# Partial sums of the first projections: added by VectorE, or copied back into PSUM and summed on there by TensorE

## The chip, the cores and the metric

The kernel runs on one core of a Trainium2 chip. The metric is the device time of one launch in microseconds, the median over runs. The engines that matter are TensorE (PE in the rows, with PEld for its weight loads), VectorE (DVE), ScalarE (ACT), and SyncE (SP), which issues the DMA transfers. GpSimd (POOL) has little to do.

## The reference

A trunk of two layers over 512 tokens of width 2048. Each layer modulates a normalised input, makes one wide projection whose columns belong to four token mixers A to D, gates each mixer's output, and projects back:

```
for i in range(DEPTH):                                    # 2 layers
    mod = silu(c) @ w_ada[i] + b_ada[i]                   # 2048 -> 3 * 2048
    shift, scale, gate = split(mod, 3)
    h = rms_norm(x, norm_w[i]) * (1 + scale) + shift      # (512, 2048)
    proj = h @ w_in[i]                                    # 2048 -> 52 column blocks of 128
    q, k, v, z of A, B, C, D = split(proj)
    y_a, y_b, y_c, y_d = window + sink, 2-D neighbourhood, dense + rotary, dilated
    y = concatenate([y_m * silu(z_m) for the four mixers])
    x = x + gate * (y @ w_out[i])                         # 2048 -> 2048
return rms_norm(x, final_norm_w)
```

All arithmetic is float32. A projection is made of float32 products split in a high and a low part (three matmuls for one step).

## The kernel before

Everything is held transposed: features on the partitions, 512 tokens on the free axis. A **step** (`step`, L213) is one 128x128 block of weights against one 128x512 input tile: three matmuls into one PSUM bank (high times high, high times low, low times high). A column block of the input projection (`kA0`, `zC1`, ...; the PSUM tile is `pj0kA0` in layer 0) needs 16 steps, one for each input tile k. There are 8 PSUM banks. Four steps make a **slot** (`slot`, L147). For each slot's weights ACT writes the high part (`wh`) and DVE the low part (`wl`); the weight blocks are laid out in memory in the order of the steps.

In layer 0 the input tiles `hh`/`hl` become ready one after the other: for each k, four tiles of `w_ada` (512 KB each) are fetched and each is reduced by DVE against `cond` (`ada_do`, L251), then `make_h` (L473) runs on DVE and ACT. So the first 16 column blocks of layer 0 are made together (`first_proj`, L495): the k's come in six groups (`GROUPS`, L62: 1, 2, 3, 4, 4 and 2 tiles). The first `KEPT` names hold a PSUM bank through all groups. The others take a bank for one group only and hand their partial sum to SBUF when the group ends (`closed`, L541): in group 0 ACT copies it into the name's half of a `b4` buffer; in groups 2 and 3 (`DEFER`) ACT copies it into a spare tile that DVE adds later (`merge`, L516); in groups 1, 4 and 5 DVE adds the bank to the SBUF tile. After group 5 the name is evacuated from SBUF.

Beside the steps run two kinds of work, placed by generators that are resumed at given positions of later slots. An **evacuation** (`evac`, L717; at most one started per slot, L159) turns a finished column block into what the mixers need: `ev_k` splits a key block for two heads (ACT copies, DVE subtractions), `ev_q`, `ev_v`, `ev_z` likewise. An attention **unit** (`unit`, L955; at most one started per slot, L154) is one head and 128 queries: scores on PE (`s`), minimum on DVE, exponential on ACT, reciprocal on DVE, scaling on ACT (`P`), transposes on PE (`pt`), copy on ACT, subtraction on DVE, and after every second unit the products with the values on PE (`o`). Layer 0 has 128 units.

What a generator may do is decided while the program is built, by counters of free buffers. The ring `b4` has 11 buffers (`BUFS`, L47): `ev_k` goes on only when `2 + RES` = 6 of them are free and takes two (L787), `ev_v` when 4 (mixers A, C) or 5 (B, D) are free and takes one (L794), a pair of units takes two; the partial sums hold one for two names. `open_proj` (L711) starts a new column block only when 3 PSUM banks are free; until then it puts in slots without steps (`idle`, L170), which carry only units and evacuations. `unit_ready` (L944) holds the next unit, and all behind it, until its head's key and value are there.

From group 1 on a scheduler may shift instructions on an engine against one another; each engine then runs its queue in order.

Of the kernel before, what the change touches and what calls it, by code (L numbers as in the profile page):

```python
# [18 lines left out]
F32 = mybir.dt.float32  # L19
F32R = mybir.dt.float32r  # L20
I32 = mybir.dt.int32
AF = mybir.ActivationFunctionType
ALU = mybir.AluOpType
# [22 lines left out]
).split()  # L46
BUFS = {"P": 4, "tmp": 4, "b4": 11, "qs": 6}  # L47
FIRST = (16, 4)
KEPT = 6
RES = 4  # L50
RES_C = 3
ORDERED = 1
# [4 lines left out]
EV = (1, 96, 4, 1, 5)  # L57
K2 = (6, 112)
DEPTH0 = 4
DEFER = (2, 3)  # L60
MERGE = (0, 0, 0, 0, 0, 3)
GROUPS = ((0,), (1, 2), (3, 4, 5), (6, 7, 8, 9), (10, 11, 12, 13), (14, 15))  # L62
NP, TP, LP, VP = (0, 1), (1, 0), (0, 1), (1, 2)
THR = (2000, 1200)
# [47 lines left out]
class Trunk:  # L112
# [98 lines left out]
            self.w_dma(self.wdma)  # L211

    def step(self, key, ps, kt, hh, hl, first, last, post=None, late=None):  # L213
        if callable(ps):
            ps = ps()
        q, i = divmod(len(self.steps), 4)
        h, lo = self.wc[q]
        c = slice(i * 128, (i + 1) * 128)
        mm = self.nc.tensor.matmul
        self.steps.append(key + (kt,))  # L220
        mm(ps, h[:, c], hh, start=first, stop=False)
        if late is None:
            mm(ps, h[:, c], hl, start=False, stop=False)
            mm(ps, lo[:, c], hh, start=False, stop=last)
            if post:
                post()
            return
        mm(ps, lo[:, c], hh, start=False, stop=False)
        late.append(lambda: mm(ps, h[:, c], hl, start=False, stop=last))
        if post:  # L230
            late.append(post)
# [263 lines left out]
    def first_proj(self):  # L495


        nc, p = self.nc, self.p
        names = ORDER[:FIRST[0]]
        part, acc = {}, {}  # L500
        rest = deque(names[KEPT:])
        merges = deque()
        spare = [0]

        def store():

            if len(self.h) > spare[0]:
                spare[0] += 1
                return p.tile([128, 512], F32, name=f"part{self.uid()}", tag="y", bufs=16), None
            if self.r_qs.free:  # L510
                return self.r_qs.get(), self.r_qs.put
            if self.r_P.free > 1:
                return self.r_P.get(), self.r_P.put
            return None

        def merge():  # L516
            _, t, u, rel = merges.popleft()
            nc.vector.tensor_tensor(t, t, u, op=ALU.add)
            if rel:
                rel()  # L520

        while rest:
            b = self.r_b4.get([128, 1024])
            left = [min(2, len(rest))]

            def rel(ring=self.r_b4, left=left):
                left[0] -= 1
                if not left[0]:
                    ring.put()
            for j in range(left[0]):  # L530
                part[rest.popleft()] = (b[:, j * 512:(j + 1) * 512], rel)
        self.w_conv(0)
        self.make_h(0, 0)
        self.rstd = self.rms_keep(self.rstd)

        def opened(n):
            if n not in acc:
                acc[n] = self.new_ps(f"pj0{n}")
            return acc[n]

        def closed(n, gi):  # L541
            end = gi + 1 == len(GROUPS)
            if n not in part:
                if end:
                    self.evq.append(self.evac(0, n, acc.pop(n)))
                return
            t, rel = part[n]
            ps = acc.pop(n)
            while end and any(m[0] == n for m in merges):
                merge()  # L550
            late = store() if gi in DEFER else None
            if gi == 0:
                nc.scalar.activation(t, ps, AF.Copy)
            elif late:
                nc.scalar.activation(late[0], ps, AF.Copy)
                merges.append((n, t, *late))
            else:
                nc.vector.tensor_tensor(t, ps, t, op=ALU.add)
            self.end_ps()
            if end:  # L560
                self.evq.append(self.evac(0, n, t, rel))

        for gi, grp in enumerate(GROUPS):
            if gi == ORDERED:
                self.ordered.close()
            tasks = self.first_tasks(GROUPS[gi + 1]) if gi + 1 < len(GROUPS) else []
            if gi == 1:
                self.start(self.tables())
            run = [(n, k) for n in names for k in grp]
            if MAJOR:  # L570
                run = [(n, k) for k in grp for n in names[:KEPT]] + [(n, k) for n in names[KEPT:] for k in grp]
            nslot = len(run) // 4
            done = 0
            for si in range(nslot):
                steps = []
                for n, k in run[4 * si:4 * si + 4]:
                    first = k == grp[0] and (n in part or gi == 0)
                    last = k == grp[-1] and (n in part or gi + 1 == len(GROUPS))
                    steps.append((("in", 0, n), lambda n=n: opened(n), k, *self.h[k], first, last,
                                  (lambda n=n: closed(n, gi)) if k == grp[-1] else None))  # L580
                self.slot(steps, [] if gi == si == 0 else None)
                upto = len(tasks) * (si + 1) // nslot
                for f in tasks[done:upto]:
                    f()
                done = upto
                for _ in range(MERGE[gi]):
                    if merges:
                        merge()
            while merges and gi + 2 == len(GROUPS) and MERGE[gi + 1] == 0:
                merge()  # L590

    def in_proj(self, l):
        self.h = []
# [613 lines left out]
```

## Time and profile before

| | us |
|---|---|
| median of 3 runs | 1900.63 (1899.38 to 1901.05) |
| the profiled execution | 1899.33 |
| its span | 1897.5 |
| PE busy in the span | 1857.0 (98%) |
| DVE busy | 1358.4 (72%) |
| ACT busy | 1078.4 (57%) |

The profiled execution is 1.3 us under the median and 1.8 us longer than its span. The busy share is an average over the whole program. What a change in one stage is worth is read from that stage: from the waits of the engine that everything else serves, here PE, and from the clock that it was granted there. Matmuls overlap in the rows (a 128x512 one lasts 0.39 us but the next starts 0.23 us later), so that starts, not durations, give the pace.

### The profile page before, as it was taken

Reading aid. Unit: us, or ns where it says so; the run is one execution under the profiler, and the core shown is the slowest. Engines: PE = TensorE matmul, PEld = TensorE weight load, DVE = VectorE, ACT = ScalarE, POOL = GpSimd, SP = SyncE. Lnnn points to the kernel's source line nnn. Section 1 sums busy time; section 2 is a strip of 40 time slices with the busy share of each in tenths; the row PEclk is TensorE's granted clock in tenths of the full one; section 3 lists DMA queues with packets and bytes.
Section 4 is the critical chain, followed back from the end, with each engine's and each line's share of the span. In section 5 each row is a group of like instructions: output and inputs, shape, how many; then the busy total and the mean of one; then the engine's idle time right before and its main releaser. Section 6 shows DMA issues by size and latency. Waiting matters only on the chain.

```text
span 1897.5 us, 26329 instructions
## 1 busy us (share of the span) xinstructions
PE 1857.0 (98%) x9256; PEld 1548.7 (82%) x9256; DVE 1358.4 (72%) x2861; ACT 1078.4 (57%) x2186; POOL 55.5 (3%) x144
## 2 busy tenths in 40 slices
PE   7899999999999999999999999999999999999997
PEld 5588888888888888888778888888888888888887
DVE  7899978788677768977775775577767666655346
ACT  5243457767777776632245773477757666654333
POOL 0110010200000000000000000110000000000000
PEclk8899999999999999999999999999999999999999
DMA  9998454252133335688833334322233342232335
GB/s 341 300 321 287 140 182 146 85 184 82 58 99 103 96 96 192 240 278 312 289 116 137 117 126 138 106 89 89 101 127 125 115 121 95 87 100 89 133 120 181
DMA packets 91459, 291.44 MB, mean 154 GB/s; under 512 B 10208, under 2 KB 17888, under 8 KB 91328
## 3 DMA queue, kind: packets, MB, share of 16 engines
q1 hardware_dynamic: 91328, 289.76, 45.1%
q8 instruction: 73, 1.20, 0.3%
q14 instruction: 58, 0.48, 0.1%
HBM read 278.57 MB, written 11.16 MB: 153 GB/s over the span
## 4 chain that ended last, share of the span: by engine, by line
PE 86%; DVE 5%; DMA 4%; ACT 2%; issue 2%; SPq 0%; DVEq 0%; ACTq 0%
PE pj1o L101 9%; PE o L101 5%; PE s L101 5%; PE pt L101 4%; PE pj0o L101 3%; PE pj0qB L101 2%; PE pj1zA L101 2%; PE pj1zC L101 2%; PE pj0kB L101 2%; PE pj1vB L101 2%; PE pj1kB L101 2%; PE pj1zB L101 2%; PE pj1qB L101 2%; PE pj1vD L101 2%; PE pj0zC L101 2%; PE pj1qC L101 2%
## 5 line engine op out<-in xcount | busy, mean ns | idle before, releaser
L101 DVE TENSOR_TENSOR wl<-wst,wh 128x512 fp32r<-128x512 f32 x556 | 383.9, 692 | 255.6 <-ACT wh L101 222.3
L101 ACT ACTIVATE wh<-wst 128x512 fp32r<-128x512 f32 x556 | 345.5, 626 | 375.0 <-PE pj1o L101 77.5
L101 ACT ACTIVATE P<-P,sm 128x512 f32<-128x512 f32 (+2 forms) x384 | 245.7, 641 | 135.7 <-DVE sm L101 133.8
L101 PE MATMUL s<-b,qs 128*128 128x512 f32 (+2 forms) x512 | 158.2, 390 | 0.2 <-DVE sm L101 0.2
L101 DVE TENSOR_TENSOR b<-pt,b 128x512 fp32r<-128x512 f32 (+2 forms) x256 | 149.4, 584 | 0.8 <-ACT b L101 0.3
L101 DVE CUSTOM_DVE_ANT_0 b<-b,cond,vec 128x1024 f32<-128x1024 f32 x96 | 123.9, 1290 | 26.9 <-DMA b<-wada 26.6
L101 PEld LDWEIGHTS pt<-cst,P 128*128 128x128 f32 x832 | 106.6, 140 | 34.6 <-ACT P L101 1.4
L101 PEld LDWEIGHTS o<-b,b 128*128 128x128 f32 x896 | 124.7, 190 | 12.2 <-DVE b L101 1.7
L101 PE MATMUL pt<-cst,P 128*128 128x128 f32 x832 | 132.4, 272 | 0.9 <-ACT P L101 0.9
L101 ACT ACTIVATE b<-pt 128x512 fp32r<-128x512 f32 (+2 forms) x256 | 129.8, 507 | 2.3
L101 DVE CUSTOM_DVE_ANT_0 b<-b,cond,half 128x1024 f32<-128x1024 f32 x96 | 124.2, 1294 | 6.2 <-DMA b<-wada 5.1
L101 PE MATMUL o<-b,b 128*128 128x256 f32 (+1 forms) x896 | 123.7, 278 | 1.4 <-DVE b L101 1.4
L101 PE MATMUL pj1o<-yh,wh 128*128 128x512 f32 (+1 forms) x304 | 108.6, 357 | 0.0
L101 PE MATMUL pj1o<-yh,wl 128*128 128x512 f32 (+1 forms) x304 | 108.3, 356 | 0.0
L101 PE MATMUL pj1o<-yl,wh 128*128 128x512 f32 (+1 forms) x304 | 108.1, 356 | 0.0
L101 PE MATMUL pj0o<-yh,wl 128*128 128x512 f32 x256 | 100.1, 391 | 0.7 <-DVE wl L101 0.6
L101 PE MATMUL pj0o<-yh,wh 128*128 128x512 f32 x256 | 100.0, 391 | 0.0
L101 PE MATMUL pj0o<-yl,wh 128*128 128x512 f32 x256 | 99.7, 389 | 0.0
L101 DVE TENSOR_TENSOR ot<-o,ot 64x256 f32<-64x256 f32 x109 | 46.0, 422 | 55.9 <-ACT ot L101 54.6
L101 DVE RECIPROCAL sm<-sm 128x1 f32<-128x1 f32 x256 | 41.4, 162 | 61.8 <-ACT P L101 59.1
L101 PEld LDWEIGHTS s<-b,qs 128*128 128x128 f32 x512 | 78.9, 191 | 2.2 <-DVE sm L101 0.4
L101 ACT ACTIVATE P<-s,sm,rq 128x512 f32<-128x512 f32 x64 | 49.8, 778 | 44.2 <-DVE sm L101 43.9
(365 smaller groups left out, 4411.7 us busy)
## 6 DMA issues: line engine op xcount, KB each, us to landing
wst<-w SPq DMA_DIRECT2D x278, 512.0 KB, 3.6
b<-wada SPq DMA_DIRECT2D x192, 512.0 KB, 6.1
T<-btab SPq DMA_DIRECT2D x16, 448.0 KB, 5.3
T<-gtab SPq DMA_DIRECT2D x16, 448.0 KB, 5.1
x<-xT SPq DMA_DIRECT2D x16, 256.0 KB, 5.3
tmp<-xT SPq DMA_DIRECT2D x16, 256.0 KB, 5.4
xs<-xn SPq DMA_DIRECT2D x16, 256.0 KB, 2.5
out<-xn SPq DMA_DIRECT2D x32, 128.0 KB, 1.8
```

Source lines behind the costliest of these rows:

```text
L101: return f(*a, **k)
```

## The change

`KEPT` goes from 6 to 5, so 11 of the first 16 names hand their sums on. These 11 no longer take a bank for each group: two banks (`rot0`, `rot1`) are held through the whole of `first_proj` and serve the 66 (name, group) places in turn. When a place ends, ACT copies its bank into the name's SBUF tile, and then copies the partial sum of the place after next from SBUF into that bank; the matmuls of that place add to what lies there (`first` is None: the first matmul doesn't start a new sum). The additions on DVE, the spare tiles, `DEFER` and `MERGE` are gone. Eleven names hold six `b4` buffers, ten held five.

```
--- before.py
+++ after.py
@@ -46,7 +46,8 @@
 ).split()
 BUFS = {"P": 4, "tmp": 4, "b4": 11, "qs": 6}
 FIRST = (16, 4)
-KEPT = 6
+KEPT = 5
+ROT = 2
 RES = 4
 RES_C = 3
 ORDERED = 1
@@ -57,8 +58,6 @@
 EV = (1, 96, 4, 1, 5)
 K2 = (6, 112)
 DEPTH0 = 4
-DEFER = (2, 3)
-MERGE = (0, 0, 0, 0, 0, 3)
 GROUPS = ((0,), (1, 2), (3, 4, 5), (6, 7, 8, 9), (10, 11, 12, 13), (14, 15))
 NP, TP, LP, VP = (0, 1), (1, 0), (0, 1), (1, 2)
 THR = (2000, 1200)
@@ -218,10 +218,11 @@
         c = slice(i * 128, (i + 1) * 128)
         mm = self.nc.tensor.matmul
         self.steps.append(key + (kt,))
-        mm(ps, h[:, c], hh, start=first, stop=False)
+        resumed = first is None
+        mm(ps, h[:, c], hh, start=bool(first), stop=False, skip_group_check=resumed)
         if late is None:
-            mm(ps, h[:, c], hl, start=False, stop=False)
-            mm(ps, lo[:, c], hh, start=False, stop=last)
+            mm(ps, h[:, c], hl, start=False, stop=False, skip_group_check=resumed)
+            mm(ps, lo[:, c], hh, start=False, stop=last, skip_group_check=resumed)
             if post:
                 post()
             return
@@ -495,29 +496,13 @@
     def first_proj(self):
 
 
-        nc, p = self.nc, self.p
+        nc = self.nc
         names = ORDER[:FIRST[0]]
         part, acc = {}, {}
         rest = deque(names[KEPT:])
-        merges = deque()
-        spare = [0]
-
-        def store():
-
-            if len(self.h) > spare[0]:
-                spare[0] += 1
-                return p.tile([128, 512], F32, name=f"part{self.uid()}", tag="y", bufs=16), None
-            if self.r_qs.free:
-                return self.r_qs.get(), self.r_qs.put
-            if self.r_P.free > 1:
-                return self.r_P.get(), self.r_P.put
-            return None
-
-        def merge():
-            _, t, u, rel = merges.popleft()
-            nc.vector.tensor_tensor(t, t, u, op=ALU.add)
-            if rel:
-                rel()
+        banks = [self.new_ps(f"rot{i}") for i in range(ROT)]
+        order = [(gi, n) for gi in range(len(GROUPS)) for n in names[KEPT:]]
+        place = {e: i for i, e in enumerate(order)}
 
...
-        def opened(n):
+        def opened(n, gi):
+            if n in part:
+                return banks[place[gi, n] % ROT]
             if n not in acc:
                 acc[n] = self.new_ps(f"pj0{n}")
             return acc[n]
 
         def closed(n, gi):
+
             end = gi + 1 == len(GROUPS)
             if n not in part:
                 if end:
                     self.evq.append(self.evac(0, n, acc.pop(n)))
                 return
+            i = place[gi, n]
+            ps = banks[i % ROT]
             t, rel = part[n]
-            ps = acc.pop(n)
-            while end and any(m[0] == n for m in merges):
-                merge()
-            late = store() if gi in DEFER else None
-            if gi == 0:
-                nc.scalar.activation(t, ps, AF.Copy)
-            elif late:
-                nc.scalar.activation(late[0], ps, AF.Copy)
-                merges.append((n, t, *late))
-            else:
-                nc.vector.tensor_tensor(t, ps, t, op=ALU.add)
-            self.end_ps()
+            nc.scalar.activation(t, ps, AF.Copy)
+            if i + ROT >= len(order):
+                self.end_ps()
+            elif order[i + ROT][0]:
+                nc.scalar.activation(ps, part[order[i + ROT][1]][0], AF.Copy)
             if end:
                 self.evq.append(self.evac(0, n, t, rel))
 
@@ -574,20 +557,15 @@
             for si in range(nslot):
                 steps = []
                 for n, k in run[4 * si:4 * si + 4]:
-                    first = k == grp[0] and (n in part or gi == 0)
+                    first = None if n in part and gi else k == 0
                     last = k == grp[-1] and (n in part or gi + 1 == len(GROUPS))
-                    steps.append((("in", 0, n), lambda n=n: opened(n), k, *self.h[k], first, last,
+                    steps.append((("in", 0, n), lambda n=n: opened(n, gi), k, *self.h[k], first, last,
                                   (lambda n=n: closed(n, gi)) if k == grp[-1] else None))
...
-                for _ in range(MERGE[gi]):
-                    if merges:
-                        merge()
-            while merges and gi + 2 == len(GROUPS) and MERGE[gi + 1] == 0:
-                merge()
```

The order of instructions moves with it. On PE, at the end of group 1 (k = 1, 2), before:

```order
L101 MATMUL pj0zA3_536<-hh0_1_333,wl8_439 128x512
L101 MATMUL pj0zA3_536<-hh0_2_402,wh8_438 128x512
L101 MATMUL pj0zA3_536<-hl0_2_403,wh8_438 128x512
L101 MATMUL pj0zA3_536<-hh0_2_402,wl8_439 128x512
L101 MATMUL pj0kA0_280<-hh0_3_492,wh12_553 128x512
L101 MATMUL g1_544<-tmp21_482,t5_411 16x512
L101 MATMUL pj0zC0_557<-hh0_1_333,wh9_463 128x512
L101 MATMUL pj0zC0_557<-hl0_1_334,wh9_463 128x512
L101 MATMUL pj0zC0_557<-hh0_1_333,wl9_464 128x512
L101 MATMUL pj0zC0_557<-hh0_2_402,wh9_463 128x512
```

Now (`rot1` holds the sum of the last name, `kC0`):

```order
L100 MATMUL rot1_246<-hh0_1_334,wh11_519 128x512
L100 MATMUL rot1_246<-hl0_1_335,wh11_519 128x512
L100 MATMUL rot1_246<-hh0_1_334,wl11_520 128x512
L100 MATMUL rot1_246<-hh0_2_397,wh11_519 128x512
L100 MATMUL rot1_246<-hl0_2_398,wh11_519 128x512
L100 MATMUL rot1_246<-hh0_2_397,wl11_520 128x512
L100 MATMUL pj0kA0_283<-hh0_3_489,wh12_550 128x512
L100 MATMUL g1_541<-tmp21_479,t5_406 16x512
L100 MATMUL pj0kA0_283<-hl0_3_490,wh12_550 128x512
L100 MATMUL pj0kA0_283<-hh0_3_489,wl12_551 128x512
```

The first matmul that reads input tile 3 (`hh0_3`) stood ahead of the group-1 steps of `zC0` to `kC0`; it now stands behind all steps of group 1.

On ACT, in group 5 (`wh` is a weight tile, `tmp<-b4` the tanh of a gate's evacuation, `qs` a query tile), before:

```order
L101 ACTIVATE wh62_1749<-wst32_1644 128x512
L101 ACTIVATE qs11_1847<-pj0qA2_306 64x512
L101 ACTIVATE qs12_1848<-pj0qA2_306 64x512
L101 ACTIVATE wh63_1775<-wst32_1644 128x512
L101 ACTIVATE tmp40_1896<-b410_245 128x512
L101 ACTIVATE tmp41_1916<-b410_245 128x512
L101 ACTIVATE tmp42_1939<-pj0vA0_283 128x512
L101 ACTIVATE wh64_1805<-wst33_1692 128x512
L101 ACTIVATE tmp43_1942<-b411_246 128x512
L101 ACTIVATE wh65_1833<-wst33_1692 128x512
L101 ACTIVATE wh66_1865<-wst34_1732 128x512
L101 ACTIVATE tmp44_1968<-b411_246 128x512
```

Now:

```order
L100 ACTIVATE b410_247<-rot0_245 128x512
L100 ACTIVATE rot0_245<-b411_248 128x512
L100 ACTIVATE tmp40_1859<-b410_247 128x512
L100 ACTIVATE b411_248<-rot1_246 128x512
L100 ACTIVATE wh63_1745<-wst32_1627 128x512
L100 ACTIVATE rot1_246<-b412_249 128x512
L100 ACTIVATE b411_248<-rot0_245 128x512
L100 ACTIVATE tmp41_1880<-b411_248 128x512
L100 ACTIVATE rot0_245<-b412_249 128x512
L100 ACTIVATE wh64_1772<-wst33_1675 128x512
L100 ACTIVATE b412_249<-rot1_246 128x512
L100 ACTIVATE tmp42_1903<-b411_248 128x512
```

Between the weight tiles and the evacuations stand a copy out of a bank (`b4..<-rot`) and a copy into it (`rot<-b4..`) for every place.

On PE, late in the input projection of layer 0, where the units of head 0 of mixer D stand (`s`, `pt`, `o` belong to units, `pj0kD2` to a projection), before:

```order
L101 MATMUL pj0kD2_6527<-hh0_3_492,wh172_6399 128x512
L101 MATMUL pj0kD2_6527<-hl0_3_493,wh172_6399 128x512
L101 MATMUL pj0kD2_6527<-hh0_3_492,wl172_6400 128x512
L101 MATMUL pt447_6569<-cst_68,P98_6491 128x128 x4
L101 MATMUL s448_6579<-b4212_6292,qs31_6038 128x512 x2
L101 MATMUL pj0kD2_6527<-hh0_4_579,wh173_6443 128x512
L101 MATMUL pj0kD2_6527<-hl0_4_580,wh173_6443 128x512
L101 MATMUL pj0kD2_6527<-hh0_4_579,wl173_6444 128x512
L101 MATMUL pj0kD2_6527<-hh0_5_644,wh173_6443 128x512
L101 MATMUL pj0kD2_6527<-hl0_5_645,wh173_6443 128x512
L101 MATMUL pj0kD2_6527<-hh0_5_644,wl173_6444 128x512
L101 MATMUL o450_6594<-b4219_6476,b4196_5779 128x256
```

Now, behind the last step of `qD3`:

```order
L100 MATMUL s435_6891<-b4226_6872,qs25_5993 128x512
L100 MATMUL s433_6883<-b4226_6872,qs25_5993 128x512
L100 MATMUL s435_6891<-b4226_6872,qs25_5993 128x512
L100 MATMUL pt437_6902<-cst_68,P97_6885 128x128 x4
L100 MATMUL s438_6908<-b4226_6872,qs25_5993 128x512 x2
L100 MATMUL pt440_6918<-cst_68,P98_6893 128x128 x4
L100 MATMUL s441_6924<-b4226_6872,qs25_5993 128x512 x2
L100 MATMUL pt443_6936<-cst_68,P99_6910 128x128 x4
L100 MATMUL s444_6944<-b4227_6873,qs26_5994 128x512 x2
L100 MATMUL o446_6953<-b4228_6900,b4193_5702 128x256
L100 MATMUL o446_6953<-b4229_6901,b4193_5702 128x256
L100 MATMUL o446_6953<-b4228_6900,b4193_5702 128x256
```

Before, twelve projection matmuls stand between the scores of one unit and those of the next; now the units of the head follow one another with none between them.

## Rows read from the trace of the kernel before

**Rows 1.** The page, part 1 and the clock line of part 2.

```profile
PE 1857.0 (98%) x9256; PEld 1548.7 (82%) x9256; DVE 1358.4 (72%) x2861; ACT 1078.4 (57%) x2186; POOL 55.5 (3%) x144
...
PEclk8899999999999999999999999999999999999999
```

**Rows 2.** Waits of PE, 0 to 400 us: total, times, longest.

```profile
PE pj0kA L101 <- ACT hh L101: 13.1, 6, 5.5
```

**Rows 3.** Waits of PE, 400 to 1898 us, the longest.

```profile
PE pj1kA L101 <- ACT hh L101: 1.6, 1, 1.6
```

**Rows 4.** Windows: PE, PEld, DVE, ACT, POOL busy, PEclk, DMA share, GB/s.

```profile
core 0: us, PE busy (x) PEld busy (x) DVE busy (x) ACT busy (x) POOL busy (x), PEclk, DMA share, GB/s
36.00:39.00 3.00, 1.59 (x7) 0.90 (x7) 2.18 (x5) 1.30 (x3) 0.00 (x0) 1.00 0.97 325
...
60.00:63.00 3.00, 0.00 (x0) 0.00 (x0) 3.00 (x7) 0.00 (x0) 0.00 (x0) 1.00 0.89 209
...
66.00:69.00 3.00, 3.00 (x6) 1.32 (x5) 1.51 (x2) 0.00 (x0) 0.00 (x0) 0.50 1.02 419
...
84.00:87.00 3.00, 2.72 (x7) 2.12 (x7) 2.22 (x4) 0.65 (x2) 0.00 (x0) 0.56 0.94 319
...
680.00:720.00 40.00, 40.00 (x212) 33.70 (x211) 26.56 (x60) 31.24 (x63) 0.00 (x0) 1.00 0.29 90
```

**Rows 5.** Timeline of PE: start, us, operation [idle before].

```profile
64.85 0.80 PE L101 MATMUL pj0kA<-hh,wh 128*128 128x512 f32 x1 [5.48 <-ACT hh L101]
...
67.98 0.63 PE L101 MATMUL pj0zC<-hl,wh 128*128 128x512 f32 x1
68.41 0.63 PE L101 MATMUL pj0zC<-hh,wl 128*128 128x512 f32 x1
```

**Rows 6.** Chain that ended last, in order of time: start, us, what.

```profile
131.63 10.88 PE pj0zA L101 x48
```

**Rows 7.** Groups of instructions, 0 to 360 us: busy, mean ns.

```profile
L101 DVE CUSTOM_DVE_ANT_0 b<-b,cond,half 128x1024 f32<-128x1024 f32 x42 | 55.2, 1313 | 0.5
...
L101 DVE TENSOR_TENSOR b<-pj0zC,b 128x512 f32<-128x512 f32 x12 | 8.2, 686 | 1.1 <-PE pj0zC L101 1.0
```

**Rows 8.** Groups of ACT, 0 to 230 us.

```profile
L101 ACT ACTIVATE wh<-wst 128x512 fp32r<-128x512 f32 x70 | 42.8, 627 | 73.5 <-PE pj0zC L101 19.3 <-PE pj0zA L101 12.1 <-PE pj0qA L101 11.8
L101 ACT ACTIVATE tmp<-b 128x512 f32<-128x512 f32 x7 | 4.4, 631 | 3.7 <-DVE y L101 2.8 <-DVE b L101 0.8
L101 ACT ACTIVATE part<-pj0zA 128x512 f32<-128x512 f32 x7 | 4.2, 597 | 11.7 <-PE pj0zA L101 9.4 <-DVE tmp L101 2.3
```

**Rows 9.** Timeline, 696 to 705 us: attention units between projection steps.

```profile
696.94 0.69 DVE L101 CUSTOM_DVE_ANT_0 P<-s,T 128x512 f32<-128x512 f32 x1
...
697.67 0.72 ACT L101 ACTIVATE P<-P,sm 128x512 f32<-128x512 f32 x1 [0.83 <-DVE sm L101]
...
698.72 0.72 ACT L101 ACTIVATE P<-P,sm 128x512 f32<-128x512 f32 x1 [0.23 <-DVE sm L101]
...
701.31 0.60 PE L101 MATMUL pt<-cst,P 128*128 128x128 f32 x4
...
701.66 0.72 PE L101 MATMUL s<-b,qs 128*128 128x512 f32 x2
...
702.22 0.39 PE L101 MATMUL pj0kD<-hh,wh 128*128 128x512 f32 x1
...
703.59 1.11 PE L101 MATMUL o<-b,b 128*128 128x256 f32 x8
...
704.54 0.39 PE L101 MATMUL pj0kD<-hh,wh 128*128 128x512 f32 x1
```

**Rows 10.** Groups of ACT by form, 600 to 720 us.

```profile
L101 ACT ACTIVATE P<-P,sm 128x512 f32<-128x512 f32 x40 | 28.9, 723 | 19.2 <-DVE sm L101 19.1
...
L101 ACT ACTIVATE b<-pt 128x512 fp32r<-128x512 f32 x18 | 10.5, 586 | 0.1
L101 ACT ACTIVATE b<-pj0kD 64x512 fp32r<-64x512 f32 x14 | 8.2, 589 | 0.2
```

## The prediction

> **What bounds the kernel now.** I read the page first: PE is busy for 1857.0 of the span's 1897.5 us, and its granted clock is below full only in the first three of 40 slices [rows 1]. Next the waits of PE. In the first 400 us it waited 13.1 us in six pieces for an input tile `hh`, the longest 5.5 us [rows 2]; from 400 us to the end no cause costs more than 1.6 us in all [rows 3], and a late window such as 680 to 720 us shows PE without a gap while DVE and ACT have 9 to 13 us of slack [rows 4]. So the kernel runs at PE's pace. DVE time that is taken away is worth something only in the first stage, until about 130 us, where PE waits for DVE's input tiles. Anything that leaves PE without ready work later is paid in full.
>
> The windows show what a wait costs beyond itself. From 60 to 63 us PE does nothing; its next matmul starts at 64.85 after 5.48 us idle, for the first reader of input tile 3 [rows 4, 5]. From 66 to 69 us the granted clock is 0.50, that is 1.2 GHz, and 128x512 matmuls start 0.43 us apart [rows 4, 5] instead of 10.88/48 = 0.227 us at 2.4 GHz [rows 6]. A shorter gap between 36 and 39 us left the clock at 1.00 [rows 4].
>
> **The change, stage one (until about 225 us).** Removed: 30 direct additions and 20 merges, 0.686 us each [rows 7], 34 us of DVE. Added on ACT: 66 copies out and 55 copies in where there were 30 copies out, so 91 more. A copy from a bank takes 0.597 us [rows 8]; into a bank there is no such row, and I take the same: 54 us, on an engine half idle here. A step is 3 x 0.227 = 0.68 us.
>
> (a) The stall at input tile 3. Before, its first reader stood in front of half of group 1; now it stands behind all of it. The 5.48 us go, and with them the slow matmuls: some eight at 0.43 instead of 0.227 and two table matmuls, about 2.6 us. Together 8. Next late is input tile 4, whose wait lies just ahead of the slow window at 84 to 87 us. Ten additions less (6.9 us) bring it earlier if DVE set its pace; the reductions that make it waited 0.5 us for DMA in 42 instructions [rows 7], but the DMA share there is 0.89 to 1.02 [rows 4]. If DVE sets it, 8 us are won; if DMA, about 4. I take -6.
>
> (b) Groups 0 and 1. A bank must be copied out and refilled while the other bank's place runs: 0.60 + 0.60 us and two hand-offs. Two hand-offs and a reciprocal lie between the exponential's end (698.39) and the scaling's start (698.72) [rows 9], so I put 0.33 us for the two as an upper estimate: 1.53 us, and some 1.65 with a weight tile (0.63 [rows 8]) now and then in front. A place of group 1 gives 2 steps, 1.36 us of cover: 11 x 0.3 = 3.3 us, and once the order on ACT puts a refill behind the next place's copy out, 1.3 us. +4.6. Group 0 has copies out alone, as before: 0.
>
> (c) Groups 2 to 4 give 2.04 and 2.72 us of cover against 1.65, or 2.3 with a weight tile in front: +1.
>
> (d) Group 5. Now the gates' evacuations come between. For each place ACT has 0.60 + 0.60, a tanh of 0.63 and half a weight tile of 0.63 [rows 8]: 2.15 us against 1.36 us of PE. 11 x 0.8 = 8.8, less the four steps of `zB1` that the order has moved in between (2.7): +6. At the low end the tanh's wait and cost nothing, 0; at the high end the six query copies ahead of the first place (6 x 0.6) add up, 12.
>
> Stage one: -6 + 4.6 + 1 + 6, about +6, between -8 and +20.
>
> **The change, stage two: what the sixth buffer moves.** Eleven names hold six `b4` buffers instead of five. The key of mixer A (needs 6 free, takes 2) therefore gets its buffers three slots later in the plan, and all units start three slots later. That alone would cost nothing. But keys wait for 6 free buffers and values only for 5, and following the counters through the code the values of the second, third and fourth pair of B's heads now take their buffers before B's first key. That key is split 24 slots later (slot 147 instead of 123), the first unit of B starts 12 slots later, six query tiles stay occupied, finished blocks hold their banks, and `open_proj` finds fewer than three free. It answers with slots without steps: 47 in layer 0 instead of 4. In the order on PE, 21 units then stand with no projection between them: 3 behind `vD0`, 3 behind `vD1`, 4 behind `vD2`, 10 behind `qD3` (head 0 and 1 of D among them, the piece shown with the change), 1 behind `zD2`. Before, nearly every unit had 12 projection matmuls, 2.7 us, beside it, and PE had no gaps [rows 4].
>
> The price of a unit without cover. PE's own part is 0.56 us for scores (701.66 to 702.22), 0.35 for transposes (701.31 to 701.66) and half of 0.95 for values (703.59 to 704.54): 1.4 us [rows 9]. ACT needs 1.77 us from the exponential's start (697.67) to the scaling's end (699.44) [rows 9] and 0.586 for the transposed copy [rows 10], 2.36 us, and a share of the output's copy; so units follow at about 2.6 us when several are open at once. PE idles 1.2 us in each: 21 x 1.2 = 25. From both sides: were the chain hidden down to ACT's bare 2 x 0.723 + 0.586 = 2.03 us, 0.6 each, 13; were units wholly serial (0.56, then 2.5 from minimum to scaling, 0.35, 0.59, 0.69, hand-offs: 5.5), 4.1 each, 86. I take the value nearest to the ACT row, since the rows of the order show the next scores ahead of the last transposes.
>
> To this come the ends. At four stretches PE waits for the last unit's chain (3.4 us from scores to transposes, less one period): 4 x 0.8 = 3. Behind `qD3` the scores of head 0 wait until a key tile of `kD0` is split (two copies of 0.589 [rows 10] and their subtractions, about 2.6 us) and the stretch ends in one more full chain: 4. Units: 25 + 3 + 4 = 32, between 15 and 95.
>
> The clock. Behind `qD3` PE works about 17 of 35 us, in pieces under 1 us. Whether 1.2 GHz is granted there no row shows; at 84 to 87 us, behind the waits for input tile 4, it was 0.56 though PE was busy 2.72 of 3 us [rows 4]. If it falls, a unit's 1.4 us of PE get longer but partly in time that PE waits anyway: 8 x 0.5 = 4, and 2 for the first projections after it. I take +6, between 0 and 25.
>
> Layer 1's plan is the old one, and the work of each instruction elsewhere is the same: 0.
>
> **Sum.** 6 + 32 + 6 = 44, on the profiled execution's 1899.3: 1943. The runs' median lies 1.3 above that execution, well inside the uncertainty of the terms; forecast 1943, for this case alone 1925 to 1962.
>
> **Rivals.**
> - The chain hides better and stage one gains: units at 13 + 3, no clock, stage one -6: 1899 + 10 = 1909 to 1925. For it: DVE and ACT have slack everywhere after 225 us [rows 4].
> - Faster: input tiles 3 and 4 both come early, so that stage one gives back its waits for `hh` after the first (9.6 of 13.1 us [rows 2]) and the slow clock behind them (4), while the 21 units cost under 10, PE finding its transposes ready each time. From a period of 1.8 us on this wins: 1890 to 1896. Against it stands ACT's 2.03 us.
> - No change: neither copies nor lost cover reach PE, 1899 to 1903. The order speaks against it.
> - The two banks make PE stop for a moment at each of 66 places and the clock falls over the first stage: groups 0, 1 and 5 have 80 steps of 0.68 us, which at 1.2 GHz last 1.28: +32 on top of the rest less what hides in waits, 1962 to 1990. Short gaps so far did not do it: at 36 to 39 us PE was busy 1.59 of 3 us and kept 1.00 [rows 4].
> - Units nearly serial: 21 x 4.1 in place of 25: 1999 and more, from 1990.
>
> The Trainium skill, TensorE: Matmul & The Clock Gate, "A second HAM failure mode: psum-queue depth-cycling", tells of a kernel that cycled through PSUM banks and whose brief idles between groups made the clock swing between its levels; this is the fourth rival's mechanism. The trace of before agrees only in that gaps cost clock (0.50 at 66 us), not that brief ones do (1.00 at 36 us); by the rule the time would be the fourth rival's.
>
> **How the numbers follow.** Forecast 0.57, hiding better 0.13, faster 0.07, no change 0.05, clock swinging 0.11, serial 0.07. A range from 1908 to 1977 holds the forecast, nearly all of the first rival and half of the fourth: about 0.8. Within 0.2% (3.8 us, about what a measurement of this kernel can tell from none) is the third rival: 0.05; faster 0.07; slower the rest, 0.88.
>
> **What would show it.** In the profile after: no wait of PE near 60 us; PE waits of some 0.3 us for ACT at places of group 1 and more in group 5; then PE full until layer 0's D blocks, four idle stretches there, the longest about 35 us with PE near half busy, its waits on ACT `P` and DVE; a lower granted clock in it; layer 1 as before. It is wrong if those stretches are absent or PE is near full in them, or if PE's waits in the first 225 us grow past 30 us.

## The result, and the profile after

The changed kernel took 1965.41 us (median of 4 runs, 1961.32 to 1968.07), the kernel before 1900.01 us beside it: ratio 1.034, 95% interval 1.0325 to 1.0356. The forecast was 1943, with a range of 1908 to 1977: slower as forecast, inside the range, and by half as much again as forecast (+65 instead of +43).

The page of the changed kernel, engine totals and clock (answers to [rows 1]):

```profile
PE 1882.8 (96%) x9256; PEld 1560.4 (80%) x9256; DVE 1334.8 (68%) x2811; ACT 1132.0 (58%) x2277; POOL 62.6 (3%) x144
...
PEclk9999999999999888999999999999999999999999
```

The span has grown by 63.5 us (1897.5 to 1961.0), PE's busy time by 25.8. So not quite half of the loss is slower or stretched PE work, the rest waits. Where it lies is read from the start of the first matmul of each stage, before and after:

```
first matmul of                     before    after   later by
value tile of C (slot 69)            235.3    241.9      6.6
first key tile of B                  338.7    341.5      2.8
output projection, layer 0           773.4    832.0     58.6
first tile, layer 1                  968.4   1031.5     63.1
end of the span                     1897.5   1961.0     63.5
```

The value 2.8 flatters: up to there 38 score matmuls had run instead of 44, since the first scores start at 276.7 us and not at 256.2; their work comes later. The first projections lost about 7 us, layer 0's attention about 52 and the turn between the layers 4 to 5; layer 1 lost nothing.

Layer 0's attention first. Waits of PE in the changed kernel from 341 to 832 us (total, times, longest):

```profile
PE pt L100 <- ACT P L100: 14.7, 8, 3.9
PE o L100 <- DVE sm L100: 4.0, 5, 1.2
PE s L100 <- DVE ot L100: 3.7, 4, 1.1
PE pt L100 <- DVE sm L100: 2.9, 3, 1.1
```

All causes sum to 29.3 us; before, the same stretch (338 to 773 us) had 0.4. 17.7 of them lie behind `qD3` (718 to 762 us). They are the waits of a unit's own chain: transposes for the scaled exponential, scores for a released bank. The windows show two pieces around the first read of input tile 3 (68 to 76 us, for further below), the end of the first projections with the banks in use, the whole attention stretch, and the ten units of head 0 and 1 of D (columns as in [rows 4]):

```profile
core 0: us, PE busy (x) PEld busy (x) DVE busy (x) ACT busy (x) POOL busy (x), PEclk, DMA share, GB/s
68.00:72.00 4.00, 2.26 (x9) 1.22 (x7) 1.43 (x3) 3.54 (x7) 0.00 (x0) 1.00 0.09 36
72.00:76.00 4.00, 2.88 (x9) 1.51 (x10) 2.44 (x4) 0.76 (x2) 0.00 (x0) 0.94 0.01 4
200.00:250.00 50.00, 48.21 (x213) 38.87 (x212) 25.89 (x39) 34.20 (x63) 0.00 (x0) 1.00 0.40 133
341.00:832.00 491.00, 461.52 (x2322) 382.36 (x2320) 328.50 (x768) 327.73 (x689) 13.78 (x39) 0.95 0.29 94
718.00:762.00 44.00, 26.30 (x112) 19.48 (x111) 28.63 (x68) 31.62 (x66) 0.00 (x0) 0.69 0.20 56
```

From 718 to 762 us PE is busy for 26.3 of 44 us at a mean clock of 0.69; before, such a window was full at 1.00 (680 to 720 us, [rows 4]). What the low clock does to a unit stands in PE's timeline, at 1.2 GHz and then, ten us later, at 2.4:

```profile
736.21 1.11 PE L100 MATMUL pt<-cst,P 128*128 128x128 f32 x4 [3.95 <-ACT P L100]
736.98 1.20 PE L100 MATMUL s<-b,qs 128*128 128x512 f32 x2
...
748.33 0.66 PE L100 MATMUL pt<-cst,P 128*128 128x128 f32 x4 [0.44 <-ACT P L100]
748.74 0.71 PE L100 MATMUL s<-b,qs 128*128 128x512 f32 x2
```

Scores of 1.20 instead of 0.71 us, transposes of 1.11 instead of 0.66: the same instructions at half the clock. Counted along PE's trace, 20 units of layer 0 stand in four stretches (3, 3, 4 and 10 units) with no projection matmul between the scores of one unit and those of the next; before, no two units stood so.

From the value tile of C to the output projection PE does the same work in both kernels. Its windows there, before and then after (columns as above):

```profile
235.30:773.40 538.10, 536.83 (x2824) 451.65 (x2822) 415.90 (x972) 381.26 (x828) 19.34 (x64) 1.00 0.37 124
```

```profile
241.90:832.00 590.10, 558.95 (x2820) 463.55 (x2819) 408.35 (x957) 387.15 (x828) 25.33 (x64) 0.96 0.33 108
```

So of the 52 us that are lost here, 30 are idle time of PE and 22 are longer busy time.

Now the first projections. Waits of PE from 20 to 262 us, then the longest wait of SyncE's DMA queue from 40 to 100 us, in the changed kernel:

```profile
PE pj0kA L100 <- ACT hh L100: 10.9, 5, 3.5
PE rot L100 <- ACT rot L100: 4.4, 8, 1.4
PE rot L100 <- DVE wl L100: 1.7, 2, 1.1
PE pj0kA L100 <- DVE hl L100: 1.4, 1, 1.4
```

```profile
SPq L449 <- DVE tmp L100: 13.5, 2, 13.3
```

The same wait in the kernel before, which the prediction had not looked at:

```profile
SPq L448 <- DVE tmp L101: 5.0, 1, 5.0
```

The banks' own waits (`rot` for ACT) are only 4.4 us. The input tiles still cost 10.9, and behind them stands SyncE: line 449 writes the table `gtab`, whose data come from a small PE matmul `g`. That matmul now stands behind all of group 1, so SyncE stood 13.3 us at the write (62.0 to 75.3 us), with the loads for the next input tiles and the weights behind it in its queue. In the windows above the DMA share falls to 0.09 and 0.01 there, and PE is busy 2.26 and 2.88 of 4 us.

### The profile page after: what moved, and what is told of

It reads as the page before. It is cut to its first block, busy times and chain, and to the rows that moved or that the text cites. A ratio compares the mean times of both kernels' runs of the same rounds, so it can differ in the third digit from the quotient of the medians.

```text
span 1961.0 us, 26341 instructions
## 1 busy us (share of the span) xinstructions
PE 1882.8 (96%) x9256; PEld 1560.4 (80%) x9256; DVE 1334.8 (68%) x2811; ACT 1132.0 (58%) x2277; POOL 62.6 (3%) x144
## 4 chain that ended last, share of the span: by engine, by line
PE 84%; DVE 6%; ACT 4%; DMA 3%; issue 2%; POOL 0%; SPq 0%; DVEq 0%; ACTq 0%
PE pj1o L100 9%; PE o L100 5%; PE s L100 5%; PE pt L100 5%; PE rot L100 4%; PE pj0o L100 4%; PE pj1zA L100 2%; PE pj1zC L100 2%; PE pj0qD L100 2%; PE pj0kB L100 2%; PE pj0vB L100 2%; PE pj0qB L100 2%; PE pj1zB L100 2%; PE pj1qD L100 2%; PE pj1qB L100 2%; PE pj0vD L100 2%
## 5 line engine op out<-in xcount | busy, mean ns | idle before, releaser
L100 PE MATMUL pt<-cst,P 128*128 128x128 f32 x832 | 137.7, 280 | 17.8 <-ACT P L100 14.7
L100 PE MATMUL o<-b,b 128*128 128x256 f32 (+1 forms) x896 | 130.2, 285 | 8.5 <-DVE sm L100 4.0
```

The source lines that it names most:

```text
L100: return f(*a, **k)
```

## The experiments

**A sixth buffer alone (e1).** The kernel before, additions and all, plus one buffer that is taken, written in one column and never read:

```diff
+        extra = self.r_b4.get([128, 1024])
+        self.nc.gpsimd.memset(extra[:, 0:1], 0.0)
+        t, rl = part["kC0"]
+        part["kC0"] = (t, lambda: (rl(), self.r_b4.put()))
```

> The kernel before with all its VectorE additions and no rotating banks; only a sixth b4 buffer is taken with the part buffers and given back with the last of them. If the plan's shift is the whole loss, the order on PE gets the same stretches without projections and the time is 1952 to 1966, with PE's first 340 us as before (within 2 us). If the copies between ScalarE and the banks cost the time, this stays at 1899 to 1905.

Measured: 1960.26 us, ratio 1.0303 (1.0286 to 1.0321). Its windows of the attention stretch and of its worst part:

```profile
core 0: us, PE busy (x) PEld busy (x) DVE busy (x) ACT busy (x) POOL busy (x), PEclk, DMA share, GB/s
341.00:827.00 486.00, 457.34 (x2298) 379.40 (x2297) 331.91 (x767) 324.00 (x681) 4.00 (x13) 0.95 0.30 104
720.00:740.00 20.00, 11.82 (x39) 8.73 (x40) 11.63 (x28) 12.56 (x27) 0.00 (x0) 0.50 0.16 46
```

PE idles 28.7 us in that stretch, and in the worst 20 us it is granted 0.50 of its clock. Not one bank copy was needed for that: the plan alone carries almost the whole loss.

**The banks with five buffers (e2).** The changed kernel, the eleventh partial sum in a `P` buffer:

```diff
         while rest:
+            if len(rest) == 1:
+                part[rest.popleft()] = (self.r_P.get(), self.r_P.put)
+                break
             b = self.r_b4.get([128, 1024])
```

> The changed kernel, with the eleventh partial sum in a P buffer, so that five b4 buffers are held as before. If the sixth buffer is the only thing that moves the plan, as the prediction has it, the old order comes back and the time is 1900 to 1908. If the build-time counters are right, which put only the first unit of head 0 two slots later here and yet leave 41 more slots without steps, there is a second way into the same plan and the time is 1950 to 1965.

Measured: 1964.36 us, ratio 1.0325 (1.0304 to 1.0346), with 19 units in stretches without projections, ten in a row. The prediction's "what the sixth buffer moves" is therefore enough for the loss and not needed for it. The first unit starts in slot 78 here (76 before, 79 in the changed kernel). I read the second way from the counters: the meter of VectorE's lag, which now misses the additions, lets the reductions start a slot earlier, and these take buffers as well. That reading was not tested by itself.

**The banks with the old plan (e4).** As e2, and mixer A's key may take its buffers at 5 free:

```diff
-        while self.r_b4.free < 2 + RES:
+        while self.r_b4.free < 2 + (3 if m == "A" else RES):
```

> The changed kernel with five b4 buffers held and mixer A's key let in at 5 free buffers instead of 6, so that the first unit starts one slot earlier than before and layer 0 has the old slots without steps. This is the banks alone. If the plan is the whole loss: no stretch without projections, layer 0's attention at full clock, 1897 to 1906. If the copies into the banks cost: 1930 or more.

Measured: 1908.09 us, ratio 1.0034 (1.0021 to 1.0048), 2 us above what was expected. No two units of layer 0 stand without projections between them. From e2 to e4 the time falls by 56 us, by an edit that lets the first unit start in slot 75 instead of 78 and brings back the old slots without steps: that is the price of the plan. The banks themselves cost 7 (1908.1 against 1900.7 beside it).

**RES = 3, with the sixth buffer, and its control (e5, e6).** `RES = 4` becomes `RES = 3` in the changed kernel and in the kernel before.

> The changed kernel, sixth buffer and all, with RES = 3 instead of 4: in both layers a key waits for 5 free buffers and a value for 4. By the counters layer 0 keeps the old slots without steps, though the first unit still starts late. If the overtaken keys are the cause, 1895 to 1906. If the sixth buffer or the late first unit costs by itself, 1930 or more.

> The kernel before with RES = 3, the control of the run above: no stretch without projections in either, so the difference of the two is the price of the banks with the rest alike. By the first 340 us of the changed kernel, 2.8 us later than before, this one is 2 to 4 us faster than the changed one with RES = 3; if the banks pay for themselves it is slower.

Measured: 1917.48 us (ratio 1.0078, 1.0064 to 1.0092) and 1902.23 us (1.0002, 0.999 to 1.0015). The time of e5 lies between its two expectations. The plan is mended with six buffers too and a first unit as late as slot 78, so neither costs tens of us. But the pair differs by 15 us, where 2 to 4 were expected; e11 takes that up.

**Values wait as long as keys (e10).** In the changed kernel, an edit meant to take away the cause that the prediction named:

```diff
-        while self.r_tmp.free < 2 or self.r_b4.free < 1 + (RES_C if m in "AC" else RES):
+        while self.r_tmp.free < 2 or self.r_b4.free < (1 + RES_C if m in "AC" else 2 + RES):
```

> The changed kernel, with values of mixers B and D waiting for 6 free buffers as the keys do, so that they no longer overtake them. By the counters 29 slots without steps in place of 55 (the kernel before has 12). If the overtaking is the whole cause, as the prediction put it, the time is 1902 to 1912. If the plan is only partly mended and each extra slot without steps costs what it did in the changed kernel, 58 us for 43, the 17 extra cost 23: 1925 to 1937.

Measured: 1944.17 us, ratio 1.0221 (1.0205 to 1.0236): above both expectations. Waits and window of its attention stretch:

```profile
PE pt L100 <- ACT P L100: 14.4, 9, 2.4
```

```profile
core 0: us, PE busy (x) PEld busy (x) DVE busy (x) ACT busy (x) POOL busy (x), PEclk, DMA share, GB/s
347.00:814.00 467.00, 448.86 (x2321) 374.68 (x2320) 328.87 (x767) 326.26 (x688) 13.48 (x39) 0.98 0.30 101
```

18 us of waits are left, and the 17 slots too many cost 2.1 us each (1944.2 against 1908.1 of e4) instead of 1.35: a price per empty slot can't be carried from one plan to another. Nor does the run isolate the overtaking. By the counters of its plan, B's first key is back in slot 120 (123 before, 147 in the changed kernel). But the value of B's first pair, which now waits for 6 free buffers too, gets its buffer in slot 144 (107 before), and B's first unit starts in slot 147 (140 before, 152 in the changed kernel). One lateness was put in place of another, and what the overtaking costs by itself is not shown.

**Fillers in the empty slots (e3, e7).** In layer 0's slots without steps, each bank that a unit takes is first written by matmuls that the real ones overwrite:

```diff
+FILL = (4, 3, 3)          # e7: (2, 1, 1)
+    def fill(self, ps, n):     # self.bare: the slot has no steps
+        if self.bare and len(getattr(self, "h", ())) == KT and self.h[-1]:
+            w = self.wc[max(self.wc)][0][:, :128]
+            for _ in range(n):
+                self.nc.tensor.eng.matmul(ps, w, self.h[-1][0], start=True, stop=True)
...
+        self.fill(sp, FILL[0])
         nc.tensor.matmul(sv, q[:, qc], keys(kk[:, 0]), start=True, stop=False)
```

> The changed kernel, and in layer 0's slots without steps each unit's banks are first written by extra matmuls that the real ones overwrite: 4 of 0.227 us ahead of the scores, 3 each ahead of the transposes and the values. They add some 50 us of PE work at most, most of it meant to lie in PE's waits. If the slow clock is what the prediction undersized, the granted clock stays nearer 1.00 from 620 to 765 us and the time falls by 5 to 20 us, to 1945 to 1960. If the clock follows from something else than PE's gaps, or waits alone set the time, the time is 1965 to 1990 and the clock as low as before.

> As the run with fillers, with 2, 1 and 1 extra matmuls in place of 4, 3 and 3: half the added PE work, some 20 us. In the first such run the clock stayed at 1.00 and PE was full, yet the time did not fall, so the fillers took what the waits and the slow clock had cost. If the slow clock cost about 25 us of its own, half the fillers leave the clock near 1.00 and the time falls to 1943 to 1955. If ScalarE's and VectorE's chains set the pace whatever PE's clock, the time stays at 1960 to 1968.

Measured: 1967.61 us (ratio 1.0351, 1.0332 to 1.037) with 182 fillers, 1957.31 us (1.0295, 1.0277 to 1.0314) with 74. Windows of the attention stretch, e3 and then e7 with the ten units:

```profile
core 0: us, PE busy (x) PEld busy (x) DVE busy (x) ACT busy (x) POOL busy (x), PEclk, DMA share, GB/s
343.00:833.00 490.00, 484.46 (x2499) 403.23 (x2497) 329.57 (x767) 326.19 (x688) 13.77 (x39) 1.00 0.28 94
```

```profile
core 0: us, PE busy (x) PEld busy (x) DVE busy (x) ACT busy (x) POOL busy (x), PEclk, DMA share, GB/s
343.00:821.00 478.00, 463.91 (x2389) 382.46 (x2389) 328.49 (x764) 326.07 (x689) 13.77 (x39) 1.00 0.29 97
718.00:762.00 44.00, 38.91 (x195) 27.96 (x194) 33.77 (x76) 34.09 (x71) 0.00 (x0) 1.00 0.19 56
```

With either, the clock is 1.00 throughout, so the low clock came from PE's gaps. The first number of fillers was too many: 182 x 0.227 = 41 us of added work used up what it saved, and its expected gain did not come. The time with 74 lies between its two expectations. The lighter run gives the price: PE is busy 463.9 us, 74 x 0.227 = 16.8 of them fillers, so 447.1 for the kernel's own work, against 461.5 in the changed kernel. By this estimate the slow clock cost 14.4 us; the same subtraction for e3 (484.5 - 41.3 = 443.2) gives 18. The stretch itself is 12.3 us shorter than without fillers (490.5 to 478.2), while PE did 16.8 us more; 8 us of it reach the end (1965.4 to 1957.3).

**The table's write on another queue (e8, e9).** The two writes of `gtab` are issued by GpSimd, in e4's kernel and in the kernel before:

```diff
-            nc.sync.dma_start(self.gtab[:, :, cs], ...
+            nc.gpsimd.dma_start(self.gtab[:, :, cs], ...
```

> The kernel with the banks and the old plan (five b4 buffers, mixer A's key let in at 5 free), with the two large writes of the table gtab issued by GpSimd instead of SyncE. In the changed kernel SyncE stood 13.3 us at such a write, whose data waits for a PE matmul that stands behind all of group 1, with the reductions' and weights' loads queued behind it, and the DMA share fell to 0.09 and 0.01 at 68 to 76 us. If that is where the first projections lost their time, the waits for input tiles 4 and 5 fall from 6.8 us to under 2 and the time is 1900 to 1905, 4 to 7 below the same kernel with SyncE. If the copies' hand-offs cost the time, it stays at 1906 to 1909.

> The kernel before with the two writes of gtab issued by GpSimd. Here SyncE stood 5.0 us at one of them, before the 5.5 us stall of PE for input tile 3 and the slow clock behind it. If that wait makes the stall, the time is 1891 to 1896, faster than the kernel before. If the loads themselves are the limit there (DMA share 0.89 to 1.02), 1898 to 1902.

Measured: e8 1896.71 us (ratio 0.997, 0.9956 to 0.9983), 11.4 below the same kernel with SyncE (e4, 1908.09) and faster than expected; e9 1895.58 us (0.9962, 0.995 to 0.9974). Windows and PE's waits of e8 in the places shown above:

```profile
core 0: us, PE busy (x) PEld busy (x) DVE busy (x) ACT busy (x) POOL busy (x), PEclk, DMA share, GB/s
68.00:72.00 4.00, 4.00 (x19) 3.17 (x18) 3.84 (x6) 3.58 (x7) 1.57 (x2) 1.00 1.03 314
72.00:76.00 4.00, 4.00 (x19) 3.29 (x19) 4.00 (x6) 2.48 (x5) 2.57 (x2) 1.00 1.02 412
```

```profile
PE pj0kA L100 <- ACT hh L100: 5.7, 3, 3.5
PE rot L100 <- ACT rot L100: 5.3, 6, 1.4
```

The DMA share is 1.03 and 1.02 instead of 0.09 and 0.01, PE is full there, and the waits for input tiles are 5.7 instead of 10.9 us (e4 has the same 10.9), while the banks' waits are no smaller (5.3). So what the first projections lost there was SyncE's stop, not the copies. In e9 the 5.48 us stall for input tile 3 is gone; in its place PE waits 2.3 us at `g`:

```profile
PE pj0kA L101 <- ACT hh L101: 8.9, 5, 3.5
PE g L101 <- DVE b L101: 2.3, 1, 2.3
```

Both runs beat both kernels, the kernel before by 0.3 and 0.4%.

**The sixth buffer again, with the queue free (e11, e12).** e5 and e6 with the same edit:

> The changed kernel with its sixth buffer, RES = 3, and the two writes of gtab issued by GpSimd. With RES = 3 alone it took 1917.5, 15 us more than the kernel before with RES = 3, where 2 to 4 were expected. If SyncE's stop at the write is most of that, as it was with five buffers (1908.1 to 1896.7), the time is 1901 to 1908. If the sixth buffer and the late first unit cost the 15 us, it stays at 1912 to 1918.

> The control: the kernel before with RES = 3 and the two writes issued by GpSimd. RES = 3 changed nothing in the kernel before and the write 5 us, so 1894 to 1898; the run above is then slower by what the banks and the sixth buffer cost when SyncE is out of the way, 4 to 10 us if the late first unit costs, 0 to 3 if it does not.

Measured: 1901.17 us (ratio 0.9996, 0.9987 to 1.0005) and 1895.43 us (0.9958, 0.9944 to 0.9971). Of e5's 15 us too many, the queue's write was most: 5.7 are left, and 1.1 with five buffers (e8 against e9). The trace of e11 has a wait of PE, at 259 us, that e8 and e12 don't have (e5 has it with 3.4 us). It is a likely part of the 5.7, which was not tested:

```profile
PE kb L100 <- POOL rq L295: 3.8, 1, 3.8
```

## Why the prediction was right, and where it was off

The 63.5 us by which the span grew are 6.6 in the first projections, 30 of idle PE and 22 of longer busy PE in layer 0's attention, and 4.5 at the turn between the layers. Forecast were 6 in the first projections, 32 of idle PE, 6 for the clock and nothing at the turn.

**Units without cover: right in the idle time, short in the busy time.** 25 + 3 + 4 = 32 us of idle PE were worked out from the order; 29.3 were measured, 17.7 of them behind `qD3` (18 is what "17 of 35 us" leaves), and half for ACT `P`. 21 units were read from the order, 20 found in the trace. e1, e2 and e4 show that this is the plan's and nearly independent of the banks. What the sum left out is that PE's own work takes longer without cover, whatever the clock: in e7, at full clock, the window from the value tile of C to the output projection has 563.5 us of busy PE, less 16.8 of fillers 546.7, against 536.8 before.

```profile
241.60:821.20 579.60, 563.51 (x2893) 465.47 (x2892) 408.83 (x956) 386.00 (x828) 25.25 (x64) 1.00 0.32 110
```

These 10 us have a likely source in [rows 9]: scores and transposes last 0.72 and 0.60 us, of which the prediction counted 0.56 and 0.35, up to the start of the next matmul. With nothing behind them the whole counts: 20 x 0.41 = 8, an estimate.

**The clock: the term that was mis-sized.** "I take +6, between 0 and 25." The mechanism stood there, and the stretch of ten units, "17 of 35 us", came out as 26.3 of 44 with the clock at 0.69. e7 prices the low clock at 14 us. The step that failed was "partly in time that PE waits anyway". Had the stretched time lain in waits, the waits would have grown by as much when e7 took it away. But e7's idle time and its fillers make 14.1 + 16.8 = 30.9 us, against 29.5 us of idle time in the changed kernel: hardly any of the 14 lay in waits. Scores and transposes stand inside a unit's chain (736.21 above), so what waits for them comes later when they are slow.

**Stage one: the sum was right by luck, its terms were wrong.** +6 was forecast, 7 measured by e4. But the copies' hand-offs were put at 4.6 + 1 + 6 and came as 4.4 us of waits, nothing of it more than 1.45 in one place: the other bank's place covers a refill better than a sum of durations with two hand-offs says. And the gain of 6 for the input tiles came to about 1: the waits for `hh` and `hl` were 12.3 us instead of 13.4. The stall at tile 3 did fall to 2.6 us, but tile 4 then waited 2.9 us for `hh` and 1.4 for `hl`, because the `g` matmul, which stood in the rows of the order that the prediction itself showed, was pushed behind group 1, and SyncE's queue behind it. The prediction followed what is queued behind PE's first reader of tile 3 and not what is queued on SyncE behind the write that needs `g`. This is worth 11.4 us with the banks (e4 to e8) and 5.3 in the kernel before (1900.84 to e9).

**Layer 1: 0 was forecast, 4 to 5 came, ahead of its first tile.** The plan of layer 1 is the old one, but the turn to it took 13.2 us from the last output matmul to the first of layer 1, not 8.1. PE's timeline there, before and after:

```profile
962.15 1.05 PE L101 MATMUL cs<-cst,tmp 128*128 128x1 f32 x8 [0.72 <-ACT tmp L101]
963.07 2.82 PE L101 MATMUL rb<-tmp,cst 128*128 128x512 f32 x6
```

```profile
1022.83 1.87 PE L100 MATMUL cs<-cst,tmp 128*128 128x1 f32 x8 [2.34 <-ACT tmp L100]
1024.56 4.45 PE L100 MATMUL rb<-tmp,cst 128*128 128x512 f32 x6
```

The last squares arrive later (2.34 us of wait instead of 0.72: VectorE's last residual sum starts 3.0 us after the last output matmul, at 1021.36, its wait ended by the residual tile's DMA; before, 0.4 us after, at 960.69), and after the wait the six matmuls `rb` take 4.45 instead of 2.82 us, at a granted clock of 0.50 instead of 1.00. The turn takes about 12 to 15.5 us in every run with a shifted plan (e1, e2, e3, e7, e10) and 8.1 or 9.8 us in all others, with and without the banks. So it goes with the plan; why the residual tiles come late in the shifted one was not tried.

**Why the plan shifts: partly right.** Five buffers instead of six do not bring it back (e2). With values that wait as long as keys, less than half is mended (e10: 1944 of 1965 to 1908), but that edit makes the values late in turn and does not price the overtaking. What the runs do show is how steep it is: a first unit in slot 75 keeps the old plan (e4), 78 or later loses it (e1, e2), unless the keys' threshold is lowered (e5). Which of the counters tips it stays open.

**The rivals.** The chain did not hide better: the waits are 29 us and not 13 + 3. The faster case needed input tiles that come early: they do so in e8, by another edit than the change. Two banks that make the clock swing: the rotation runs from 33 to 233 us, and from 200 to 250 us the clock is 1.00 though PE stood 1.8 us, 1.45 of it at once for a bank. What the prediction quoted of the Trainium skill, TensorE: Matmul & The Clock Gate, "A second HAM failure mode: psum-queue depth-cycling", is a kernel whose brief idles between groups came often; here PE waited for a bank in 8 of 66 places, so the cycling alone did not do it, and no run here shows that kernel's case. Serial units: no, since the waits are 29 and not 86 us.

**Readings that do not hold.** The clock line of [rows 1] is below its top digit in the first two slices, not three. The 0.5 us ahead of the reductions in [rows 7] names no releaser, so it need not be DMA. The fourth rival's 80 steps at half the clock would add 80 x 0.60 = 48 us, not 32. And that brief gaps cost no clock holds at 36 us only: the 0.56 at 84 to 87 us [rows 4] stands behind waits of at most 0.92 us.

## What to carry to other kernels

A change that takes one buffer more, or makes a planner's meter cheaper, is first a change of the order: hold the buffer in the old kernel without using it (e1) and see what that costs before pricing the new instructions. When a matmul is moved, follow its result into every queue that waits for it: a DMA that stands at the head of SyncE's queue for a late table holds up all loads behind it (13.3 us here), and moving the table's two writes to another queue was the only edit here that beat both kernels (1895.6 and 1896.7 against 1900.8). And a gap on PE is charged twice where the clock falls with it: 29 us of waits brought 14 us of slower matmuls.

## What the runs showed of the hardware

A 128x512 float32 copy by ScalarE into a PSUM bank takes about what one out of it takes: 601 ns against 589 on average in the changed kernel, between 40 and 230 us (group rows of ACT):

```profile
L100 ACT ACTIVATE b<-rot 128x512 f32<-128x512 f32 x58 | 34.0, 589 | 18.6 <-PE rot L100 18.4
L100 ACT ACTIVATE rot<-b 128x512 f32<-128x512 f32 x54 | 32.4, 601 | 1.3
```

The sums went on in the bank after such a copy, with no first-matmul flag; each bank had been opened by a flagged matmul in group 0. Between 140 and 235 us PE is busy 92.9 of 95 us there, against 95.0 before. PE also kept its full clock with fillers in its gaps even where 5.1 of 44 us stayed idle (e7, 718 to 762 us), against a mean of 0.69 without them and 17.7 us idle.
